# RWKV inverse in a hybrid retention and RWKV-7 block: both directions' units of a step inverted together, their matrix loaded by four transfers

## The chip, the cores and the metric

One core of one Trainium2 chip runs the kernel as one program. The core has a matrix engine (PE, with its weight loads PEld), a vector engine (DVE), an activation engine (ACT), a general engine (POOL) and a queue engine (SP) that here issues most DMAs; in the traces here each executes its own instructions in the order in which they stand in the built program. Time is device time in microseconds of the whole launch, the median of several runs; "the profiled execution" is a further run with the hardware profiler on, which has a time of its own.

## The reference: what is computed

A transformer block for 1024 latent tokens and 256 context tokens, width 1024: an FFN, a mixer of two parallel branches (retention with 4 heads of 128, and RWKV-7 with 8 heads of 64), a second FFN, a final norm. The branch that the change concerns is the RWKV scan. It runs in two directions (z = 0 and 1), over the context first and then over the latents with the state that the context left:

```python
def step(s, inp):
    rt, wt, kt, vt, at, bt = inp
    sa = jnp.einsum('zbhvk,zbhk->zbhv', s, at)
    s_new = s * wt[..., None, :] + sa[..., :, None] * bt[..., None, :] + vt[..., :, None] * kt[..., None, :]
    y = jnp.where(is_fwd, einsum(s_new, rt), einsum(s, rt))
    return s_new, y
```

The kernel computes it in chunks of 64 tokens. Within a chunk the recurrence through `sa` is a unit triangular system of 64 equations for each head, so every chunk needs the inverse of a 64 by 64 triangular matrix.

## The kernel before, in words

**Stages.** `tile_kernel` builds, in this order: the start and the first FFN; the RWKV projections (`rkv`); the RWKV scan (`recurrences`, L1073); the remaining projections of the mixer (`fill`, L1128, made of `qkvg`, L765, and `gates`, L796); the retentions (L1136); the output projections (`merge_rwkv`, `merge_ret`, `residual`, whose PSUM tiles are `rwps` and `ops`); the second FFN (PSUM tiles `p` and `psd`) and the final norm. The instructions are not run in that order: a scheduler places each engine's instructions when the program is built, by dependencies and by when it reckons buffers and engines free. An instruction of a later stage can thus stand among those of an earlier one, if its tiles have memory that is free.

**The scan.** There are 10 steps, each with two units (z = 0 and 1) of 128 tokens, so 20 units. A unit goes through three parts.
- `prep` (L868) loads r, k, v, kk and the decay of 128 tokens, forms two prefix products (`w`, `wi`, L893), the scaled operands `ar` and `bk`, and with 32 matmuls the Gram matrices `gps`; DVE masks them into `g` (L926, L930).
- `inverse` (L958) inverts the 32 diagonal blocks of 32 by 32 (8 heads, 2 chunks, 2 halves) by substitution. The blocks are copied from `g` to DRAM (`scr<-g`, L969, four transfers), and read back by one transfer of 512 KB (`invn<-scr`, L970), whose source has a first dimension of stride 0: the 32 blocks stand four times over the 128 partitions. Partition group j solves for the rows j, j+4, ... ACT copies those into `invx` (L972). Then 30 times two DVE operations, a product into `invt` (L976) and a sum into `invx` (L977). Four memsets write the diagonal (L980), and the result goes to DRAM (`scr<-invx`, L981) and back into `g` (`g<-scr`, L983).
- `join` (L985) makes the 64 by 64 inverse of two 32 by 32 ones: for each of two chunks e, 8 transposes (`tps`), an ACT copy, 8 products (`hps`), an ACT copy, 8 products (`xps`), and a DVE copy into `g` (L1002).
- `chain` (L1004) is the recurrence proper. For each chunk: `q` from the state S and from `wv` (L1018, L1020), an ACT copy, `u` with the inverse (L1025), an ACT copy, the state's update (L1030, POOL L1032, DVE L1034), and the output (L1037, L1039 or L1041). `readout` (L1044) normalises the outputs of a page that both directions have visited and stores them (L1071).

**Order and buffers of the scan.** `recurrences` prepares and inverts units 0, 1 and 2 ahead (`ready`), and behind step s the units 2s+3 and 2s+4. The tiles `ar`, `g`, `bt`, `wv` and `pc` have a ring of four buffers; the loads of `prep` have one buffer each; `invn`, `invx` and `invt` have two buffers each.

**The fill.** `qkvg` has 40 blocks of 24 matmuls (`fps`, L207 to L209): 16 with 512 tokens, 8 with 256, 16 with 512. `gates` has 32 blocks with 512 tokens. A block's weights come by two DMAs of 256 KB (`wraw`), which ACT and POOL split in two (L196, L197). Of a head's four blocks in `qkvg`, the first two (q and rk) are rotated with the tables `cos` and `sin` (L774, L789 to L793). The blocks' results go through a tile `gs` with two buffers.

**Memory.** The tiles of the scan are taken from the low end of the on-chip memory upwards, those of the fill from the high end downwards. In the built program the last tile of the scan (a small one of `readout`) ends at byte 163,040 of a partition, and the lowest tile of the fill (`cos`, 2 KB) begins at byte 165,376.

Of the kernel before, what the change touches and what calls it, by code (L numbers as in the profile page):

```python
# [11 lines left out]
F32 = mybir.dt.float32  # L12
F32R = mybir.dt.float32r
AF = mybir.ActivationFunctionType
ALU = mybir.AluOpType
PSUM = bass.MemoryType.PSUM

P = 128
# [823 lines left out]
def ab(c):  # L842

    return 0 if c % 2 else 64
# [6 lines left out]
class Rwkv(Mixer):  # L851
# [103 lines left out]
            nc.scalar.activation(wv[r, :, e], ps[r], AF.Copy)  # L955
        return {"p": p, "ar": ar, "g": g, "bt": bt, "wv": wv, "pc": pc}

    def inverse(self, g, eng, tmp):  # L958


        nc = self.nc
        d0, d1 = (self.scr.tile([2, 2, 8, 32, 32], F32, tag="scr%d" % i, name="scr%d" % i) for i in range(2))
        n = tmp.tile([P, 32, 32], F32, tag="invn", name="invn", bufs=2)
        x = tmp.tile([P, 8, 32], F32, tag="invx", name="invx", bufs=2)
        t = tmp.tile([P, 72], F32, tag="invt", name="invt", bufs=2)
        ef = [(e, f, slice(ab(e) + 32 * f, ab(e) + 32 * f + 32)) for e in range(2) for f in range(2)]
        blk = lambda e, r: g[r, e, :, :, r].rearrange("i a b t -> i (a b) t")
        for e, f, r in ef:
            nc.sync.dma_start(out=d0[f, e].rearrange("q i t -> i q t"), in_=blk(e, r))  # L969
        nc.sync.dma_start(out=n, in_=d0.rearrange("f e q i t -> (f e q) (i t)").unsqueeze(0).to_broadcast([4, 32, 1024]))  # L970
        for j in range(4):
            nc.scalar.activation(x[32 * j:32 * j + 32], n[32 * j:32 * j + 32, j::4], AF.Copy)  # L972
        for i in range(1, 31):
            w, m = 31 - i, (i + 3) // 4
            tv = t[:, :m * w].rearrange("q (r c) -> q r c", c=w)
            eng.tensor_tensor(out=tv, in0=x[:, :m, i:i + 1].to_broadcast([P, m, w]), in1=n[:, i:i + 1, i + 1:].to_broadcast([P, m, w]), op=ALU.mult)  # L976
            eng.tensor_tensor(out=x[:, :m, i + 1:], in0=x[:, :m, i + 1:], in1=tv, op=ALU.add)  # L977
        for j in range(4):
            r = slice(32 * j, 32 * j + 32)
            eng.memset(x[r].rearrange("q k t -> q (k t)")[:, j::36], 1.0)  # L980
            nc.sync.dma_start(out=d1[:, :, :, j::4].rearrange("f e q k t -> (f e q) k t"), in_=x[r])  # L981
        for e, f, r in ef:
            nc.sync.dma_start(out=blk(e, r), in_=d1[f, e].rearrange("q i t -> i q t"))  # L983

    def join(self, g, tmp, pq):  # L985

# [86 lines left out]
    def recurrences(self, ctx):  # L1073
        nc, tc = self.nc, self.tc
        pool = lambda nm, bufs, **k: ctx.enter_context(tc.tile_pool(name=nm, bufs=bufs, **k))
        tmp, ring, ct = pool("btmp", 1), pool("bring", 4), pool("bct", 2)
        self.scr = pool("bscr", 2, space=bass.MemoryType.DRAM)
        pp, pc = pool("bpp", 2, space=PSUM, side="right"), pool("bpc", 2, space=PSUM)
        items = [(s, z) for s in range(10) for z in range(2)]
        un, seen = {}, set()  # L1080

        def ready(i):
            s, z = items[i]
            un[i] = self.prep(s, z, ring, tmp, pp)
            self.inverse(un[i]["g"], nc.vector, tmp)

        for i in range(3):
            ready(i)
        late, joined = [], set()

        def join(i):
            if i in un and i not in joined:
                joined.add(i)
                self.join(un[i]["g"], tmp, pc)

        for s in range(10):
            old, ys, late, runs = late, [], [], []
            for z in range(2):
                u = un[2 * s + z]
                p, y = u["p"], None  # L1100
                if p < 8:
                    y = ct.tile([P, 512], F32, tag="y", name="y", bufs=2)
                    if p in seen:
                        nc.scalar.dma_start(out=y, in_=self.dram["y", p])
                    ys.append((p, y))
                runs.append(self.chain(u, z, y, p not in seen, s == 9, ct, pc))
                join(2 * s + z)
                next(runs[z])
            for p, y in old:
                self.readout(p, y, ct, pc)  # L1110
            for z, x in enumerate(runs):
                next(x)
                if z == 0:
                    join(2 * s + 2)
            for p, y in ys:
                if p in seen:
                    late.append((p, y))
                else:
                    nc.scalar.dma_start(out=self.dram["y", p], in_=y)
                    seen.add(p)  # L1120
            for i in (2 * s + 3, 2 * s + 4):
                if i < 20:
                    ready(i)
            join(2 * s + 3)
        for p, y in late:
            self.readout(p, y, ct, pc)
# [422 lines left out]
```

## Time and profile before

| | us |
|---|---|
| median of 3 runs (lowest, highest) | 3290.09 (3285.87, 3291.71) |
| profiled execution, its own time | 3270.48 |
| its span, first to last instruction | 3268.7 |
| first matmul of the scan's chain (L1018) | 1276.1 |
| first and last load of `invn` | 1302.6 and 2183.4 |
| last matmul of the fill (L209, `fps`) | 2249.2 |
| last matmul of the chain (L1037) | 2301.3 |
| first matmul of `rwps`, of `ops`, of the second FFN (`p`) | 2343.9, 2464.5, 2562.9 |

A row of a view names a line of the kernel, an engine, an operation and its tiles as "written<-read", with buffer numbers left out. "x600: 144/216/1962" is a count with the least, the median and the longest duration in ns. In a row of groups, "202.5, 340 |" is the busy time in us and the mean of one in ns. A row of a stretch of time gives its limits and length in us, then for each engine the busy time with the number of instructions, then the granted share of the matrix engine's clock, the share of the DMA engines' time and GB/s. A row of the chain of work (what ended last, followed back) gives start, length and what it was. Matmuls overlap in the records, so a busy matrix engine isn't one at its peak.

### The profile page before, as it was taken

To read this page: it belongs to the slowest core of one execution; us is meant where nothing else is said; L and a number is where in the kernel's file an instruction comes from. 1 tells how busy PE (TensorE), PEld (TensorE's weight loads), DVE (VectorE), ACT (ScalarE), POOL (GpSimd) and SP (SyncE) were. 2 spreads that over 40 slices of the span, in tenths; PEclk is the share of its full clock that TensorE was granted. 3 is DMA by queue.
4 is the path that set the end of the run, shared out by engine and by line. 5 is a ranking of instruction groups with operands and counts; after the bars stand their busy time and mean duration, and the time that the engine had idled before them with its cause. 6 is when DMAs were issued, how large, how long until landed. Compare 5 with 4: busy or idle time off the path is not lost.

```text
span 3268.7 us, 47408 instructions
## 1 busy us (share of the span) xinstructions
PE 3037.0 (93%) x17879; PEld 2525.8 (77%) x17879; DVE 2006.5 (61%) x3826; ACT 1050.2 (32%) x1790; POOL 950.0 (29%) x768
## 2 busy tenths in 40 slices
PE   8999999999999998788889888888899899999998
PEld 4888888888887786677667677777787688888877
DVE  4876666444448874788666766755766776675012
ACT  5211111111115474334333333333423533333221
POOL 2111111111113313333332322332223533333442
PEclk9999999999999998888888888798899899999999
DMA  5432222111116246556444444534545244448651
GB/s 207 135 94 91 90 91 81 40 39 39 33 39 233 92 174 202 131 154 173 120 121 110 120 131 110 166 92 124 160 152 163 84 140 146 132 136 288 229 174 61
DMA packets 504557, 416.57 MB, mean 127 GB/s; under 512 B 92264, under 2 KB 401448, under 8 KB 504328
## 3 DMA queue, kind: packets, MB, share of 16 engines
q1 hardware_dynamic: 487776, 401.65, 40.5%
q10 hardware_dynamic: 16552, 11.90, 1.2%
q8 instruction: 141, 2.31, 0.3%
q14 instruction: 88, 0.72, 0.1%
HBM read 309.89 MB, written 99.35 MB: 125 GB/s over the span
## 4 chain that ended last, share of the span: by engine, by line
PE 66%; DVE 15%; DMA 11%; issue 3%; ACT 2%; SPq 2%; POOL 1%; DVEq 0%; ACTq 0%; POOLq 0%
PE psd L207 5%; PE psd L208 5%; PE psd L209 5%; DMA invn<-scr 5%; PE p L208 4%; PE p L209 4%; PE p L207 4%; PE psg L209 3%; DVE invt L976 3%; PE psu L208 3%; PE psg L208 3%; PE psu L209 3%; PE psu L207 3%; PE psg L207 3%; DVE invx L977 2%
## 5 line engine op out<-in xcount | busy, mean ns | idle before, releaser
L197 POOL TENSOR_TENSOR wlo<-wraw,whi 128x512 fp32r<-128x512 f32 (+1 forms) x246 | 437.8, 1790 | 1333.0 <-ACT whi L196 1251.5
L389 DVE SCALAR_TENSOR_TENSOR h<-psd,g,h 128x512 f32<-128x512 f32 (+1 forms) x504 | 313.6, 657 | 273.0 <-PE psd L209 272.8
L196 ACT ACTIVATE whi<-wraw 128x512 fp32r<-128x512 f32 (+1 forms) x246 | 193.8, 804 | 369.3 <-DMA wraw<-in_w_in_dram 88.7
L207 PE MATMUL fps<-uh,whi 128*128 128x512 f32 (+1 forms) x576 | 247.3, 430 | 23.9 <-ACT whi L196 15.0
L207 PE MATMUL p<-v,fac 128*128 128x512 f32 x616 | 242.0, 393 | 11.2 <-ACT v L42 6.1
L209 PE MATMUL fps<-uh,wlo 128*128 128x512 f32 (+1 forms) x576 | 245.5, 427 | 3.3 <-POOL wlo L197 3.3
L208 PE MATMUL p<-v,fac 128*128 128x512 f32 x616 | 242.0, 393 | 4.6 <-DVE v L43 4.6
L208 PE MATMUL fps<-ul,whi 128*128 128x512 f32 (+1 forms) x576 | 243.5, 423 | 0.1
L976 DVE TENSOR_TENSOR invt<-invx,invn 128x60 f32<-128x60 f32 (+5 forms) x600 | 202.5, 340 | 66.1 <-issue 31.0
L209 PE MATMUL p<-v,fac 128*128 128x512 f32 x616 | 241.4, 392 | 0.0
L977 DVE TENSOR_TENSOR invx<-invx,invt 128x60 f32<-128x60 f32 (+5 forms) x600 | 193.6, 325 | 26.3 <-DMA rsw<-gs 6.0
L207 PE MATMUL psd<-hh,whi 128*128 128x512 f32 (+1 forms) x528 | 189.8, 360 | 7.0 <-DVE h L389 6.9
L207 PE MATMUL psg<-uh,whi 128*128 128x512 f32 (+1 forms) x528 | 188.8, 358 | 0.9 <-ACT whi L196 0.9
L208 PE MATMUL psg<-ul,whi 128*128 128x512 f32 (+1 forms) x528 | 189.1, 358 | 0.4 <-POOL ul L259 0.4
L209 PE MATMUL psg<-uh,wlo 128*128 128x512 f32 (+1 forms) x528 | 188.8, 358 | 0.0
L207 PE MATMUL psu<-uh,whi 128*128 128x512 f32 (+1 forms) x528 | 187.7, 356 | 0.2 <-ACT whi L196 0.2
L208 PE MATMUL psu<-ul,whi 128*128 128x512 f32 (+1 forms) x528 | 187.6, 355 | 0.0
L208 PE MATMUL psd<-hl,whi 128*128 128x512 f32 (+1 forms) x528 | 187.1, 354 | 0.0
L209 PE MATMUL psu<-uh,wlo 128*128 128x512 f32 (+1 forms) x528 | 187.1, 354 | 0.0
L209 PE MATMUL psd<-hh,wlo 128*128 128x512 f32 (+1 forms) x528 | 186.8, 354 | 0.0
L207 PEld LDWEIGHTS fps<-uh,whi 128*128 128x128 f32 x576 | 123.5, 214 | 53.0 <-ACT whi L196 17.4
L43 POOL TENSOR_TENSOR fac<-draw,fac 128x512 fp32r<-128x512 f32 x88 | 114.3, 1302 | 138.9 <-ACT fac L42 137.8
(365 smaller groups left out, 7059.6 us busy)
## 6 DMA issues: line engine op xcount, KB each, us to landing
wraw<-in_w_in_dram SPq DMA_DIRECT2D x144, 256.0 KB
modw<-in_w_mod_dram SPq DMA_DIRECT2D x112, 256.0 KB
fraw<-in_ffn_w_gate_dram SPq DMA_DIRECT2D x88, 256.0 KB
hd<-d_hid SPq DMA_DIRECT2D x44, 512.0 KB
draw<-in_ffn_w_down_dram SPq DMA_DIRECT2D x88, 256.0 KB
wraw<-in_ffn_w_gate_dram SPq DMA_DIRECT2D x22, 512.0 KB
wraw<-in_ffn_w_up_dram SPq DMA_DIRECT2D x22, 512.0 KB
wraw<-in_ffn_w_down_dram SPq DMA_DIRECT2D x22, 512.0 KB
```

The costliest lines, as they stand in the source:

```text
L43: eng.tensor_tensor(out=v[1], in0=x, in1=v[0].bitcast(F32), op=ALU.subtract)
L196: nc.scalar.activation(hi[:, s], raw, AF.Copy)
L197: nc.gpsimd.tensor_tensor(out=lo[:, s], in0=raw, in1=hi[:, s].bitcast(F32), op=ALU.subtract)
L207: mm(ps, w[0][:, ws], x[0][xs], start=start, stop=False)
L208: mm(ps, w[0][:, ws], x[1][xs], start=False, stop=False)
L209: mm(ps, w[1][:, ws], x[0][xs], start=False, stop=stop)
L389: nc.vector.scalar_tensor_tensor(out=hs, in0=ps, scalar=gates()[v][:, m:m + 1], in1=hs, op0=ALU.mult, op1=ALU.add)
L976: eng.tensor_tensor(out=tv, in0=x[:, :m, i:i + 1].to_broadcast([P, m, w]), in1=n[:, i:i + 1, i + 1:].to_broadcast([P, m, w]), op=ALU.mult)
L977: eng.tensor_tensor(out=x[:, :m, i + 1:], in0=x[:, :m, i + 1:], in1=tv, op=ALU.add)
```

## The change

`inverse` takes both units of a step. `invn`, `invx` and `invt` get one more dimension u of two, and each of the 60 substitution operations covers both units: 60 operations of double size for a step, where there were 120. `invn` keeps its size in all, with one buffer of 8 KB for two of 4 KB. `invx` and `invt` keep two buffers and double: 2 KB for 1 KB, and 576 bytes for 288, so the scan's tiles take 2 x (1024 + 288) = 2,624 bytes more of each partition. The load of `invn` becomes four transfers of 128 KB for each unit, one for each partition group, with 32 rows each. Copies, stores and memsets stay as they were for each unit, but the memsets are shared. `recurrences` prepares two whole steps ahead (units 0 to 3), and behind step s the step s+2 (units 2s+4 and 2s+5).

```diff
-    def inverse(self, g, eng, tmp):
+    def inverse(self, gs, eng, tmp):
...
-        n = tmp.tile([P, 32, 32], F32, tag="invn", name="invn", bufs=2)
-        x = tmp.tile([P, 8, 32], F32, tag="invx", name="invx", bufs=2)
-        t = tmp.tile([P, 72], F32, tag="invt", name="invt", bufs=2)
+        n = tmp.tile([P, 2, 32, 32], F32, tag="invn", name="invn")
+        x = tmp.tile([P, 2, 8, 32], F32, tag="invx", name="invx", bufs=2)
+        t = tmp.tile([P, 144], F32, tag="invt", name="invt", bufs=2)
...
-        nc.sync.dma_start(out=n, in_=d0.rearrange("f e q i t -> (f e q) (i t)").unsqueeze(0).to_broadcast([4, 32, 1024]))
-        for j in range(4):
-            nc.scalar.activation(x[32 * j:32 * j + 32], n[32 * j:32 * j + 32, j::4], AF.Copy)
+        for u, g in enumerate(gs):
...
+            for j in range(4):
+                nc.sync.dma_start(out=n[32 * j:32 * j + 32, u].rearrange("q i t -> q (i t)"), in_=d0.rearrange("f e q i t -> (f e q) (i t)"))
+            for j in range(4):
+                nc.scalar.activation(x[32 * j:32 * j + 32, u], n[32 * j:32 * j + 32, u, j::4], AF.Copy)
         for i in range(1, 31):
             w, m = 31 - i, (i + 3) // 4
...
-            eng.tensor_tensor(out=x[:, :m, i + 1:], in0=x[:, :m, i + 1:], in1=tv, op=ALU.add)
+            eng.tensor_tensor(out=x[:, :, :m, i + 1:], in0=x[:, :, :m, i + 1:], in1=tv, op=ALU.add)
...
-        def ready(i):
-            s, z = items[i]
-            un[i] = self.prep(s, z, ring, tmp, pp)
-            self.inverse(un[i]["g"], nc.vector, tmp)
-
-        for i in range(3):
-            ready(i)
+        def ready(s):
+
+            for z in range(2):
+                un[2 * s + z] = self.prep(s, z, ring, tmp, pp)
+            self.inverse([un[2 * s + z]["g"] for z in range(2)], nc.vector, tmp)
+
+        ready(0)
+        ready(1)
...
-            for i in (2 * s + 3, 2 * s + 4):
-                if i < 20:
-                    ready(i)
+            if s < 8:
+                ready(s + 2)
```

In the built program of the change the last tiles of the scan (small tiles of `readout`, and 32 bytes of the second buffer of its tile `ysq`) end at byte 165,664; `cos`, the lowest tile of the fill, still begins at 165,376. The two share 288 bytes. The order in which the scheduler then places the instructions differs from the order before at the places below.

On SP, where `cos` is loaded for the first time: before, among the last stores of the RWKV projections (`d_td`, `d_na`, `d_r`), ahead of the scan's first unit.

```order
L717 DMA d_r<-rs 128x1024
L680 DMA d_td_66<-l2o 128x2x256
L774 DMA cos<-in_cst_cos_dram 128x512
L774 DMA sin<-in_cst_sin_dram 128x512
L194 DMA wraw<-in_w_in_dram 128x4x128
```

On SP in the change, the same load (L989 is the last return of an inverse to `g`, L1296 reads what `readout` stored).

```order
L987 DMA scr_15358<-invx 256x1x32 x2
L989 DMA g<-scr_15358 32x8x32 x4
L1296 DMA t_20089<-d_rw_83 128x128
L1296 DMA t_20089<-d_rw_86 128x128
L1296 DMA t_20089<-d_rw_89 128x128
L194 DMA wraw<-in_w_rwkv_o_dram 128x4x256 x4
L194 DMA wraw<-in_w_ret_o_dram 128x4x256
L774 DMA cos<-in_cst_cos_dram 128x512
L774 DMA sin<-in_cst_sin_dram 128x512
L789 DMA rsw<-gs 32x512
```

The load of `cos`, and with it all that follows it in `qkvg`, has moved from ahead of the scan to behind its last inverse.

On PE, in the middle of the scan before: a chain's `q` (L1018, L1020), a join (L998, L1001, L995) and a `prep` (L923), with matmuls of the fill (`fps`) between them.

```order
L1018 MATMUL q<-S_10082,ar 128x128 x4
L1020 MATMUL q<-wv,g 64x64 x3
L998 MATMUL hps<-tt,g 32x32 x8
L1020 MATMUL q<-wv,g 64x64 x5
L923 MATMUL gps<-ar,bk 128x128 x8
L207 MATMUL fps<-uh,whi 128x512
L208 MATMUL fps<-ul,whi 128x512
L209 MATMUL fps<-uh,wlo 128x512
```

On PE in the change, the same kind of place (lines of `join` and `chain` are six higher: L1024 and L1026 are `q`, L1004, L1007 and L1001 the join).

```order
L1024 MATMUL q<-S_10082,ar 128x128 x4
L1026 MATMUL q<-wv,g 64x64 x5
L923 MATMUL gps<-ar,bk 128x128 x8
L1007 MATMUL xps<-g,tt 32x32 x8
L1001 MATMUL tps<-ident,g 32x32 x8
L1026 MATMUL q<-wv,g 64x64 x3
L1004 MATMUL hps<-tt,g 32x32 x8
L947 MATMUL btps<-ident,bk 128x128 x8
```

On PE in the change, the end of the scan (L1043 is the chain's output, L1069 the readout).

```order
L1031 MATMUL u<-qa,g 64x64 x16
L1043 MATMUL q<-wv,g 64x64 x16
L1069 MATMUL ytps<-ident,y 128x128 x8
L207 MATMUL fps<-uh,whi 128x512
L208 MATMUL fps<-ul,whi 128x512
L209 MATMUL fps<-uh,wlo 128x512
```

In the change no `fps` stands between the first `q` and the last readout: 48 of the fill's 1,728 (two blocks) stand ahead of the scan, and 1,680 behind it.

On SP in the change, between one pair's substitution and the next (L974 loads `invn`, L987 and L989 store and return the pair before, L972 copies `g` of the next pair's second unit).

```order
L974 DMA invn<-scr_12901 32x1024
L987 DMA scr_12308<-invx 256x1x32 x4
L987 DMA scr_12322<-invx 256x1x32 x2
L989 DMA g<-scr_12308 32x8x32 x4
L987 DMA scr_12322<-invx 256x1x32 x2
L974 DMA invn<-scr_12901 32x1024 x2
L989 DMA g<-scr_12322 32x8x32 x4
L974 DMA invn<-scr_12901 32x1024
L972 DMA scr_12915<-g 32x8x32 x4
L974 DMA invn<-scr_12915 32x1024 x4
```

The next pair's first load stands ahead of the stores of the pair before, and its second unit's copy and loads behind their return. On DVE the second unit's masks (L926) stand behind the first join's copies (L1008) of the pair before.

More of the change, by code (lines that the diff above doesn't have):

```diff
@@ L956, in prep @@
         return {"p": p, "ar": ar, "g": g, "bt": bt, "wv": wv, "pc": pc}
-    def inverse(self, g, eng, tmp):
+    def inverse(self, gs, eng, tmp):
         nc = self.nc
-        d0, d1 = (self.scr.tile([2, 2, 8, 32, 32], F32, tag="scr%d" % i, name="scr%d" % i) for i in range(2))
-        n = tmp.tile([P, 32, 32], F32, tag="invn", name="invn", bufs=2)
-        x = tmp.tile([P, 8, 32], F32, tag="invx", name="invx", bufs=2)
-        t = tmp.tile([P, 72], F32, tag="invt", name="invt", bufs=2)
+        n = tmp.tile([P, 2, 32, 32], F32, tag="invn", name="invn")
+        x = tmp.tile([P, 2, 8, 32], F32, tag="invx", name="invx", bufs=2)
+        t = tmp.tile([P, 144], F32, tag="invt", name="invt", bufs=2)
@@ L966, in inverse @@
         ef = [(e, f, slice(ab(e) + 32 * f, ab(e) + 32 * f + 32)) for e in range(2) for f in range(2)]
[L967 to L970, printed above, removed]
-        for j in range(4):
-            nc.scalar.activation(x[32 * j:32 * j + 32], n[32 * j:32 * j + 32, j::4], AF.Copy)
+        blk = lambda g, e, r: g[r, e, :, :, r].rearrange("i a b t -> i (a b) t")
@@ new lines, in inverse @@
+        d1s = []
+        for u, g in enumerate(gs):
+            d0, d1 = (self.scr.tile([2, 2, 8, 32, 32], F32, tag="scr%d%d" % (u, i), name="scr%d" % i) for i in range(2))
+            d1s.append(d1)
+            for e, f, r in ef:
+                nc.sync.dma_start(out=d0[f, e].rearrange("q i t -> i q t"), in_=blk(g, e, r))
+            for j in range(4):
+                nc.sync.dma_start(out=n[32 * j:32 * j + 32, u].rearrange("q i t -> q (i t)"), in_=d0.rearrange("f e q i t -> (f e q) (i t)"))
+            for j in range(4):
+                nc.scalar.activation(x[32 * j:32 * j + 32, u], n[32 * j:32 * j + 32, u, j::4], AF.Copy)
@@ L973, in inverse @@
         for i in range(1, 31):
             w, m = 31 - i, (i + 3) // 4
-            tv = t[:, :m * w].rearrange("q (r c) -> q r c", c=w)
-            eng.tensor_tensor(out=tv, in0=x[:, :m, i:i + 1].to_broadcast([P, m, w]), in1=n[:, i:i + 1, i + 1:].to_broadcast([P, m, w]), op=ALU.mult)
-            eng.tensor_tensor(out=x[:, :m, i + 1:], in0=x[:, :m, i + 1:], in1=tv, op=ALU.add)
+            tv = t[:, :2 * m * w].rearrange("q (u r c) -> q u r c", u=2, c=w)
+            eng.tensor_tensor(out=tv, in0=x[:, :, :m, i:i + 1].to_broadcast([P, 2, m, w]), in1=n[:, :, i:i + 1, i + 1:].to_broadcast([P, 2, m, w]), op=ALU.mult)
@@ L978, in inverse @@
+            eng.tensor_tensor(out=x[:, :, :m, i + 1:], in0=x[:, :, :m, i + 1:], in1=tv, op=ALU.add)
         for j in range(4):
             r = slice(32 * j, 32 * j + 32)
[L980 to L983, printed above, removed]
+            eng.memset(x[r].rearrange("q u k t -> q u (k t)")[:, :, j::36], 1.0)
@@ L985, in join @@
+        for u, g in enumerate(gs):
+            for j in range(4):
+                nc.sync.dma_start(out=d1s[u][:, :, :, j::4].rearrange("f e q k t -> (f e q) k t"), in_=x[32 * j:32 * j + 32, u])
+            for e, f, r in ef:
+                nc.sync.dma_start(out=blk(g, e, r), in_=d1s[u][f, e].rearrange("q i t -> i q t"))
     def join(self, g, tmp, pq):
@@ L1078, in recurrences @@
         pp, pc = pool("bpp", 2, space=PSUM, side="right"), pool("bpc", 2, space=PSUM)
-        items = [(s, z) for s in range(10) for z in range(2)]
         un, seen = {}, set()
-        def ready(i):
-            s, z = items[i]
-            un[i] = self.prep(s, z, ring, tmp, pp)
-            self.inverse(un[i]["g"], nc.vector, tmp)
-        for i in range(3):
-            ready(i)
+        def ready(s):
[4 more added lines that the diff above has]
+        ready(1)
         late, joined = [], set()
```

## The prediction

> **What bounds the kernel now.** I read the stretches of time first: they cut the span where the fill ends, where the first output projection starts and where the second FFN starts.
>
> ```profile
> 1276.00:2249.00 973.00, 836.88 (x6908) 693.97 (x6908) 678.39 (x1784) 345.73 (x669) 332.73 (x328) 0.85 0.48 129
> 2249.00:2344.00 95.00, 72.29 (x674) 65.66 (x672) 61.37 (x175) 41.31 (x79) 26.20 (x18) 0.82 0.52 161
> 2344.00:2563.00 219.00, 206.79 (x1003) 171.51 (x1003) 142.31 (x262) 74.88 (x113) 75.07 (x37) 0.98 0.49 153
> 2563.00:3269.00 706.00, 679.44 (x3000) 561.07 (x3000) 352.86 (x476) 240.66 (x396) 261.26 (x194) 0.97 0.48 156
> ```
>
> The scan and the fill share 973 us. The matrix engine looks 86% busy there, but its records overlap, so next comes the chain of work over 1276 to 2301 us, then the inverse's tiles and its transfers.
>
> ```profile
> by line: DMA invn<-scr 14.8%; DVE invt L976 9.0%; DVE invx L977 7.9%; issue 5.8%; PE fps L207 3.8%; PE fps L209 3.7%; PE fps L208 3.5%; PE gps L923 2.5%; PE u L1025 2.2%; PE q L1018 2.2%; PE q L1020 2.2%; ACT invx L972 1.8%; DMA scr<-g 1.6%
> L976 DVE TENSOR_TENSOR invt<-invx,invn x600: 144/216/1962, 1316.4 to 2222.0; 128x60 f32<-128x60 f32 x30, 128x48 f32<-128x48 f32 x19, 128x28 f32<-128x28 f32 x18, 128x52 f32<-128x52 f32 x10
> L970 SPq DMA_DIRECT2D invn<-scr x20: 562/576/632, 1302.6 to 2183.4; - x20
> 1302.60 12.03 DMA invn<-scr
> 1340.61 11.27 DMA invn<-scr
> ```
>
> The chain's largest item is the load of `invn`, 12.03 us from issue to landing; the substitution follows. The matrix multiplications of the fill have 3.5 to 3.8% a line: the stage is paced by the scan's latency, and the fill runs in its holes. 20 loads lie between 1302.6 and 2183.4 us, 46.4 us a unit, so a step takes 92.7 us before. That the fill costs nothing of its own is what the kernel before lives on.
>
> **The change part by part.** What decides is not in the substitution. The scan's tiles now reach 288 bytes into the place of `cos`, so `cos` is loaded when the last readout has done with that memory. The first head's q and rk blocks hold both `gs` buffers until they are rotated with `cos`; so after two blocks the fill stands, and the order of PE shows it: 48 of 1,728 matmuls ahead of the scan, none in it, 1,680 behind. The rest follows from three durations: the scan alone, the fill alone, and the tail.
>
> *The scan alone: a step.* Its DVE work comes first.
>
> ```profile
> L976 DVE TENSOR_TENSOR invt<-invx,invn 128x60 f32<-128x60 f32 (+5 forms) x600 | 202.5, 340 | 66.1 <-issue 31.0 <-ACT invx L972 16.2 <-DMA wraw<-in_w_in_dram 3.9
> L977 DVE TENSOR_TENSOR invx<-invx,invt 128x60 f32<-128x60 f32 (+5 forms) x600 | 193.6, 325 | 26.3 <-DMA rsw<-gs 6.0 <-issue 4.6
> L926 DVE TENSOR_TENSOR g<-gps,c_msk 128x512 f32<-128x512 f32 x64 | 43.0, 686 | 5.5 <-PE gps L923 4.6
> L1034 DVE TENSOR_TENSOR S<-S,u 64x256 f32<-64x256 f32 x70 | 29.1, 416 | 11.1 <-PE u L1030 9.8
> L793 DVE TENSOR_TENSOR gs<-gs,rsw 128x512 f32<-128x512 f32 x16 | 17.3, 1081 | 0.0
> L1002 DVE COPY g<-xps 32x256 f32<-32x256 f32 x38 | 15.8, 416 | 38.0 <-PE xps L1001 31.2 <-issue 6.2
> L792 DVE TENSOR_TENSOR gs<-gs,cos 128x512 f32<-128x512 f32 x16 | 15.2, 948 | 15.5 <-ACT invx L972 8.9 <-DMA rsw<-gs 4.0 <-DMA wraw<-in_w_in_dram 2.5
> ```
>
> An operation of the substitution has a median of 216 ns and a least of 144, which is nearly all fixed cost. Twice the elements add about the difference: 288 ns, between 216 and 432. A pair takes 60 x 0.288 = 17.3 us; before, 120 operations took 120 x 0.216 = 25.9 us, and by the means 39.6. So the edit itself saves 8.6 to 22 us of DVE a step. The rest of DVE is 678.4 - 202.5 - 193.6 - 17.3 - 15.2 (the fill's own) = 249.8 us, 25.0 a step. Of it two state updates (0.8), four masks (2.7) and four copies of the join (1.7) stand between two substitutions by the order of DVE. The stretch from the start to the end of a substitution is thus 17.3 + 25.0 - 5.2 = 37.1 us.
>
> Between two substitutions nothing overlaps, because `invn` has one buffer now, and because the second unit's masks stand behind the first join.
>
> ```profile
> L969 SPq DMA_DIRECT2D scr<-g x80: 318/443/2003, 1299.1 to 2180.2; - x80
> L981 SPq DMA_DIRECT2D scr<-invx x80: 549/588/2413, 1354.9 to 2224.7; - x80
> 1274.16 3.37 DMA rsw<-gs
> 1357.30 1.92 DMA scr<-invx
> 1359.69 2.23 DMA g<-scr
> 1614.67 3.47 DMA wraw<-in_w_in_dram
> 1621.00 1.97 DMA rsw<-gs
> 1651.42 1.64 DMA scr<-g
> 2251.68 0.69 PE L998 MATMUL hps<-tt,g 32*32 32x32 f32 x16
> 2259.70 1.05 PE L998 MATMUL hps<-tt,g 32*32 32x32 f32 x16 [3.84 <-ACT tt L996]
> 2259.28 0.36 ACT L996 ACTIVATE tt<-tps 32x256 f32<-32x256 f32 x1
> 2262.97 0.41 DVE L1002 COPY g<-xps 32x256 f32<-32x256 f32 x1
> ```
>
> One load's issue (0.58), four stores (4 x 0.588), their landing (1.92), and the return (2.23, and one issue more) make 7.5 us. The join of a chunk took 2263.38 - 2259.28 = 4.1 us from the first ACT copy on, where no fill stood between, and its transposes 0.7: two chunks 9.6. Then state and masks 3.5, the copies of `g` 4 x 0.443 + 1.64 = 3.4, four loads 4 x 0.576 + landing, ACT 0.4. The new load is not in the trace; it lies between a 64-KB transfer (1.97 to 3.37) and the 512-KB one (12.03). I take 3 us for the last 128 KB, near the 256-KB weights (3.47). Sum: 7.5 + 9.6 + 3.5 + 3.4 + 2.3 + 3 + 0.4 = 29.7 us.
>
> [...]
>
> A step takes 37.1 + 29.7 = 67 us, for 92.7 before. The bounds are DVE's bare work (42) and 92.7.
>
> *The scan's place.* Its first `q` is at 1276 as before. The first substitution needs two units: between 1302.6 and 1340.6 for the last load; I take 1322. It starts at 1325 and ends at 1362, the tenth nine steps later: 1362 + 9 x 67 = 1965.
>
> ```profile
> L1018 PE MATMUL q<-S,ar x320: 272/275/582, 1276.1 to 2291.9; 128*128 128x128 f32 x128, 128*64 128x128 f32 x32
> 2284.75 2.07 PE L1018 MATMUL q<-S,ar 128*128 128x128 f32 x8 [2.52 <-DVE y L1041]
> 2288.76 0.59 ACT L1022 ACTIVATE qa<-q 64x512 f32<-64x512 f32 x1 [2.17 <-PE q L1020]
> 2271.74 2.97 DMA y<-d_bv
> 2274.84 1.27 POOL ysq L1070
> ```
>
> From there to the fill's restart: the joins of both units (7.5 + 2 x 9.6 = 27); one and a half chunks of chain (three matmul groups of 1 to 2 us, two ACT copies of 0.6, the state's sum 0.8: 7 each) and the last readout's arithmetic, 21 in all as an estimate from such pieces; its two loads and POOL products (8.5) and its store (3); `cos` with the first rotation (11). That is 70 us, bounds 50 and 100. The fill restarts at 2035.
>
> The new wait sits in SP's queue: behind `cos` stand the rotation's transfers, the weights of `qkvg` and all stores of its blocks, and on PE everything from the third block on. Nobody in the scan waits for it. No cover is left for the fill: it must be paid after the scan.
>
> *The fill alone.* No stretch shows it; the nearest is `ops`, 16 blocks of the same 24 matmuls with streamed weights.
>
> ```profile
> L207 PE MATMUL ops<-uh,whi x128: 388/389/628, 2464.5 to 2557.0; 128*128 128x512 f32 x128
> L209 PE MATMUL fps<-uh,wlo x576: 274/389/796, 1261.9 to 2249.2; 128*128 128x512 f32 x171, 128*128 128x256 f32 x21
> L207 PE MATMUL p<-v,fac x616: 387/389/792, 2562.9 to 3000.1; 128*128 128x512 f32 x154
> 1529.69 4.24 DMA ul<-d_u
> ```
>
> (2557.0 - 2464.5) / 16 = 5.8 us a block. Two blocks ran ahead, two more fit in PSUM while `cos` is awaited: 60 wide blocks make 348 us, 8 of half width 35 (23 to 46), three changes of the token group, whose operands come in transfers of some 4 us, 8 each. Sum 407, bounds 375 and 450: to 2442.
>
> *The tail.* Before, 2249.2 to 2562.9 = 314 us lay between the last `fps` and the second FFN, of which the chain and its readouts held a part up to 2344; from there it was 219. Now these are over earlier, and the retentions, which need the fill, remain: 255. The second FFN starts at 2697 and takes its 706: the end is at 3403, 134 us behind 3268.7. Against the profiled execution's own 3270.5 that is 3405; the median of the runs shown is 19.6 above it, so 3290 + 134 = 3424.
>
> **The rivals.** *Cold matrix engine, slower still.* Alone, the scan leaves it long pauses: the same 16 matmuls took 0.69 us behind dense work and 1.05 after 3.84 us of idling, and the clock granted in the scan is 0.85 even with the fill. If chain and masks wait for it too, 10 to 15 us a step come on top: 9 x 12 = 108, 3532. [...]
>
> *Faster.* A substitution saves more than the fill then costs, if a step alone takes under 67 - 134 / 9 = 52 us: stores, joins and loads must hide beneath DVE's 42 us. At 47 the time is 3290 + 134 - 180 = 3244. For it: long waits of the step before are those for the fill's matmuls in front. Against: one `invn` buffer, and SP's and DVE's order above.
>
> *The fill is not displaced*, as the diff alone reads: then 25.7 us a step are saved, 9 x 25.7 = 231, 3059. The order of PE excludes it all but wholly.
>
> **How the numbers follow.** Forecast 0.77; cold 0.14; faster 0.06; not displaced 0.01; 0.02 for a step near 52 us, which ends within 0.2% (6.6 us, about what a measurement here can tell from no change). Steps of 60 and 73 us move the forecast by 60, the fill by 35, tail and start by 30 each: together some 90. The range goes 114 down to 3310 and 106 up, to the cold case at 3530. Faster 0.07, same 0.02, slower 0.91.
>
> **What would show it.** `fps` must be absent between the first `q` and the last readout, with the matrix engine under half busy there; the loads of `invn` must recur every 67 us and land within about 4; `cos` must be issued near 2020; `fps` then runs dense for 400 us. I am wrong if a step is under 52 us, or if `fps` ends before 2330.

## The result, and the profile after

The changed kernel takes 3513.1 us (median of four runs, 3508.1 to 3525.8), the kernel before 3288.0 on the same chip: 1.070 times as long, 95% interval 1.065 to 1.075. The forecast was 3424, in a range of 3310 to 3530: the time lies inside it, near its upper end, and the kernel is 225 us slower where 134 were forecast. The profiled execution has a span of 3508.9 us, for 3268.7 before.

The stretches of time of the changed kernel, cut at the end of the scan's matmuls, the return of the fill, its end, and the start of the second FFN (start:end, length, busy time of PE, PEld, DVE, ACT and POOL, granted TensorE clock, DMA share, GB/s):

```profile
1276.00:2071.00 795.00, 558.33 (x5607) 502.19 (x5604) 454.10 (x1135) 231.83 (x467) 145.22 (x183) 0.59 0.30 75
2071.00:2097.00 26.00, 2.21 (x9) 1.43 (x8) 14.34 (x31) 5.38 (x9) 11.90 (x7) 0.56 0.55 169
2097.00:2537.00 440.00, 402.23 (x1732) 324.96 (x1733) 41.24 (x52) 122.96 (x216) 204.21 (x153) 0.94 0.54 166
2537.00:2803.00 266.00, 239.58 (x1247) 203.52 (x1246) 166.48 (x362) 97.21 (x162) 79.98 (x40) 0.95 0.45 143
2803.00:3509.00 706.00, 679.28 (x3000) 560.95 (x3000) 351.69 (x476) 240.55 (x396) 260.90 (x194) 0.97 0.48 156
```

Before, scan and fill shared 973 us. Now the scan has 795 for itself, in which TensorE gets 0.59 of its clock, and behind it the fill takes 440 at 0.94. The last stretch is as long as before, to the microsecond.

The instructions of the inverse, of `cos` and of the fill in the changed kernel (count, least, median and greatest duration in ns, first and last start):

```profile
L974 SPq DMA_DIRECT2D invn<-scr x80: 312/420/1423, 1296.5 to 1973.0; - x80
L980 DVE TENSOR_TENSOR invt<-invx,invn x300: 179/264/1974, 1318.5 to 2005.1; 128x120 f32<-128x120 f32 x30, 128x56 f32<-128x56 f32 x20, 128x96 f32<-128x96 f32 x20, 128x60 f32<-128x60 f32 x10
L774 SPq DMA_DIRECT2D cos<-in_cst_cos_dram x2: 333/336/340, 2096.5 to 2187.6; - x2
L207 PE MATMUL fps<-uh,whi x576: 278/389/797, 1261.4 to 2536.8; 128*128 128x512 f32 x171, 128*128 128x256 f32 x21
```

`cos` is loaded at 2096.5, behind the scan, and the `fps` matmuls end at 2537 where they ended at 2249. An operation of the pair has a median of 264 ns for twice the elements (216 before). How little of it goes with the elements, single operations of the kernel before show: 0.17 us with 8 elements a partition (at 1642.59), 0.23 with 68 (at 1719.51). Two waits in the scan changed places (engine and line, what it waited for, total, times, longest). In the kernel before:

```profile
ACT invx L972 <- DMA invn<-scr: 155.2, 19, 15.2
DVE g L1002 <- PE xps L1001: 31.2, 12, 7.2
```

and in the changed kernel:

```profile
DVE g L1008 <- PE xps L1007: 101.7, 23, 10.2
ACT invx L976 <- DMA invn<-scr: 64.8, 42, 8.4
```

ACT's copies wait 64.8 us for the load of `invn`, where they waited 155.2. DVE's copies of the join wait 101.7 us for TensorE, where they waited 31.2.

### The profile page after: what moved, and what is told of

Same layout as the page of the kernel before. It is cut to its first block, busy times and chain, and to the rows that moved or that the text cites. A ratio compares the mean times of both kernels' runs of the same rounds, so it can differ in the third digit from the quotient of the medians.

```text
span 3508.9 us, 46957 instructions
## 1 busy us (share of the span) xinstructions
PE 3121.0 (89%) x17879; PEld 2625.1 (75%) x17879; DVE 1798.3 (51%) x3186; ACT 1045.0 (30%) x1783; POOL 956.9 (27%) x768
## 3 DMA queue, kind: packets, MB, share of 16 engines
q1 hardware_dynamic: 488976, 401.65, 37.1%
## 5 line engine op out<-in xcount | busy, mean ns | idle before, releaser
L207 PE MATMUL fps<-uh,whi 128*128 128x512 f32 (+1 forms) x576 | 228.0, 397 | 42.9 <-ACT whi L196 21.9
L209 PE MATMUL fps<-uh,wlo 128*128 128x512 f32 (+1 forms) x576 | 226.2, 393 | 8.2 <-POOL wlo L197 8.0
L208 PE MATMUL fps<-ul,whi 128*128 128x512 f32 (+1 forms) x576 | 226.1, 393 | 0.9 <-DMA ul<-d_u 0.7
L207 PEld LDWEIGHTS fps<-uh,whi 128*128 128x128 f32 x576 | 114.4, 199 | 72.4 <-ACT whi L196 28.8
L923 PE MATMUL gps<-ar,bk 64*128 64x128 f32 (+1 forms) x640 | 99.4, 400 | 66.5 <-POOL ar L905 26.6
L1038 POOL TENSOR_TENSOR S<-S,pc 64x256 f32<-64x256 f32 x76 | 56.5, 743 | 332.5 <-PE q L1024 303.2
```

Source lines behind the costliest of these rows:

```text
L207: mm(ps, w[0][:, ws], x[0][xs], start=start, stop=False)
L208: mm(ps, w[0][:, ws], x[1][xs], start=False, stop=False)
L209: mm(ps, w[1][:, ws], x[0][xs], start=False, stop=stop)
L923: nc.tensor.matmul(pss[h][:, j, e, xs], bk[r, h0 + j, e], ar[r, h0 + j, e, xs], start=True, stop=True)
L1038: nc.gpsimd.tensor_tensor(out=S[hc[h], :, hc[h]], in0=S[hc[h], :, hc[h]], in1=pc[hc[h], e::2].unsqueeze(2).to_broadcast([64, 4, 64]), op=A ...
```

## The experiments

Two theories stood against each other at first. *Displacement*: the time is lost because 288 bytes push the fill out of the scan. *The pair*: the paired inverse with its one `invn` buffer is slow of itself. "First to last substitution" is the time from the first start of an `invt` operation to the last, and holds nine steps and most of a tenth.

**1. The change, made to fit.** One buffer of `invt`, which should make nothing wait, since DVE alone writes and reads it, one operation behind the other:

```diff
-        t = tmp.tile([P, 144], F32, tag="invt", name="invt", bufs=2)
+        t = tmp.tile([P, 144], F32, tag="invt", name="invt")
```

> The changed kernel with one buffer of invt instead of two: 576 bytes less a partition, so that the scan's last tiles end at byte 165,088, below the start of cos (165,376); the order of PE has 1,668 fps matmuls inside the scan again. Displacement theory (what costs is that the fill is pushed behind the scan, by 288 bytes): the time falls below the kernel before. PE then sets the pace: about 400 us of fps and some 430 us of the scan's own matmuls at a full clock, 830 to 880 us between the first q and the last, where before has 973: 3290 - 100 = about 3190 us, between 3140 and 3240. Rival (the paired inverse with its one invn buffer is slow of itself): 3290 us or more, up to 3510.

3177.1 us, 0.9686 of the kernel before (0.9672 to 0.9700). Its `fps` and its substitutions:

```profile
L207 PE MATMUL fps<-uh,whi x576: 278/389/795, 1262.3 to 2092.6; 128*128 128x512 f32 x171, 128*128 128x256 f32 x21
L980 DVE TENSOR_TENSOR invt<-invx,invn x300: 171/274/1837, 1339.0 to 2171.8; 128x120 f32<-128x120 f32 x30, 128x56 f32<-128x56 f32 x20, 128x96 f32<-128x96 f32 x20, 128x60 f32<-128x60 f32 x10
```

The fill runs through the scan again and is done by 2093. The `invt` operations wait for ACT (10.8 us) and for two loads (6.1 us), and for no operation of DVE. The scan is longer than where it runs alone (832.8 us from first to last substitution, for 686.6), and still the kernel is some 335 us faster than the changed one. Displacement is what costs.

**2. The kernel before, made not to fit.** Padding alone, no instruction more:

```diff
-        t = tmp.tile([P, 72], F32, tag="invt", name="invt", bufs=2)
+        t = tmp.tile([P, 400], F32, tag="invt", name="invt", bufs=2)
```

> The kernel before with invt padded from 72 to 400 elements, so that its scan tiles end at byte 165,664 like those of the changed kernel; not one instruction is added. Displacement theory: fps leaves the scan, cos is issued behind the last readout, and the time is 150 to 300 us above the kernel before: 3440 to 3590 us (the scan alone 75 to 85 us a step, then 430 us of fps as in the changed kernel). Rival (the paired inverse is what costs): within 1% of the kernel before, 3260 to 3320 us.

3561.0 us, 1.0856 (1.0833 to 1.0879).

```profile
L774 SPq DMA_DIRECT2D cos<-in_cst_cos_dram x2: 333/336/340, 2140.7 to 2233.0; - x2
L207 PE MATMUL fps<-uh,whi x576: 277/389/796, 1262.9 to 2584.0; 128*128 128x512 f32 x171, 128*128 128x256 f32 x21
```

`cos` comes late and `fps` ends 335 us later than before. The same displacement, without any of the change, costs 283 us.

**3 and 4. Where the step is.** The same padding, with 364 and with 360 elements for 400: an overlap of 32 bytes, and a gap of 32.

> The kernel before with invt padded from 72 to 364 elements: the scan's last tile ends at byte 165,408, 32 bytes above the start of cos. Displacement as a step (any overlap displaces the whole fill): the same time as with 288 bytes of overlap, 3540 to 3580 us. Rival (the price grows with the bytes, or is one of the padding itself): between the kernel before and that, under 3450 us.

> The kernel before with invt padded from 72 to 360 elements: the scan's last tile ends at byte 165,344, 32 bytes below the start of cos, and TensorE's order is word for word that of the kernel before. Displacement as a step: 3265 to 3295 us, as the kernel before. Rival (the padding has a price of its own, from other addresses): over 3310 us.

364 elements: 3559.3 us, 1.0867 (1.0836 to 1.0898). 360 elements: 3280.1 us, 1.000 (0.9982 to 1.0018). The price is a step: 32 bytes cost what 288 cost, and the padding itself nothing.

**5. The load alone.** The kernel before, with only the load in four transfers:

```diff
-        nc.sync.dma_start(out=n, in_=d0.rearrange("f e q i t -> (f e q) (i t)").unsqueeze(0).to_broadcast([4, 32, 1024]))
+        for j in range(4):
+            nc.sync.dma_start(out=n[32 * j:32 * j + 32].rearrange("q i t -> q (i t)"), in_=d0.rearrange("f e q i t -> (f e q) (i t)"))
```

> The kernel before with only the load of invn in four transfers. If the broadcast's 10 to 12 us is on the path while the fill runs beside it, some 8 us a unit go, less what PE's queue takes back: 3200 to 3270 us. Rival (the load is hidden behind the other unit's substitution and the wait for PE): within 0.5% of the kernel before, 3275 to 3305 us.

3174.2 us, 0.9680 (0.9665 to 0.9695): better than either theory had it, and not to be told from the fitting change.

```profile
L977 DVE TENSOR_TENSOR invt<-invx,invn x600: 154/216/1964, 1301.9 to 2089.4; 128x60 f32<-128x60 f32 x29, 128x48 f32<-128x48 f32 x19, 128x28 f32<-128x28 f32 x13, 128x70 f32<-128x70 f32 x10
```

First to last substitution takes 787.5 us here and took 905.6 before: 118 us gone, of which the time shows 104. The load was on the path even with the fill beside it.

**6. The pair with the old load.** The fitting kernel of experiment 1, with one broadcast transfer for each unit:

```diff
-            for j in range(4):
-                nc.sync.dma_start(out=n[32 * j:32 * j + 32, u].rearrange("q i t -> q (i t)"), in_=d0.rearrange("f e q i t -> (f e q) (i t)"))
+            nc.sync.dma_start(out=n[:, u].rearrange("q i t -> q (i t)"), in_=d0.rearrange("f e q i t -> (f e q) (i t)").unsqueeze(0).to_broadcast([4, 32, 1024]))
```

> The fitting kernel (one buffer of invt) with the old broadcast load, one for each unit. If the load is on the path once the fill runs beside it: 5 to 8 us more a step than the fitting kernel, so 50 to 80 us above it. Rival (PE is full in the scan and hides the load): within 0.5% of the fitting kernel.

3322.1 us, 1.0127 (1.0111 to 1.0142): 145 us above experiment 1, about twice what was expected, and slower than the kernel before. ACT's wait for the load, here:

```profile
ACT invx L975 <- DMA invn<-scr: 185.5, 20, 13.6
```

and in experiment 1:

```profile
ACT invx L976 <- DMA invn<-scr: 47.9, 37, 6.9
```

138 us more of waiting stand beside 145 us more of time. That fits a load which, in a pair, nothing covers.

**7. The pair alone, where the scan runs alone.** The padding of experiment 2 and the load of experiment 5 together; against the changed kernel the pairing is undone, and with it the order in which units are prepared and the one buffer of `invn`.

> The kernel before with both the padded invt (400 elements, the scan's tiles end at byte 165,664 as in the changed kernel) and the load in four transfers: against the changed kernel only the pairing of the substitution is undone. If the pairing pays where the scan runs alone (it takes 8 to 22 us of DVE a step): 3540 to 3561 us, little below the padded kernel. Rival (in the scan alone the short load is worth as much as the pairing, since the load is on the path and a single unit starts earlier): 3470 to 3520 us, at or below the changed kernel's 3513.

3414.1 us, 1.0414 (1.0380 to 1.0448), below both ranges. The same stretch of time of this kernel:

```profile
1320.00:1920.00 600.00, 493.51 (x4983) 445.65 (x4983) 482.37 (x1653) 206.43 (x416) 118.34 (x155) 0.60 0.35 86
```

and of the changed kernel:

```profile
1320.00:1920.00 600.00, 418.50 (x4308) 375.44 (x4307) 350.62 (x888) 184.00 (x370) 102.11 (x136) 0.59 0.30 76
```

With single units DVE is busy 482 of 600 us, with pairs 351, at the same granted clock. The pair does its substitution in fewer operations and then lets DVE stand: in the scan alone it is 2.8% the worse (1.0703 / 1.0414), some 95 us. With the fill beside it (experiments 1 and 5), it gains nothing and loses nothing in the whole time.

The traces show where those 95 us lie. With single units, 15 of the 19 gaps between one substitution's last operation and the next one's first are under 1.5 us: while DVE solves one unit, the next is made ready. In the changed kernel the nine gaps are 35.9 us in the mean. Two units take 63.2 us with single units, and a pair takes 73.2.

**8 and 9. Is it the single buffer?** The prediction put the pair's gaps down to the one buffer of `invn`, and to the order of the second unit's masks. The changed kernel with two buffers (the fill is displaced anyway), and experiment 7 with one (padded to the same end):

```diff
-        n = tmp.tile([P, 2, 32, 32], F32, tag="invn", name="invn")
+        n = tmp.tile([P, 2, 32, 32], F32, tag="invn", name="invn", bufs=2)
```

> The changed kernel with two buffers of invn for one (8 KB more a partition; the fill is behind the scan anyway). The padded kernel before with the four-transfer load took 3414 us, so the pairing costs 99 us, 10 a step. If that is the single buffer of invn, as the prediction had it (the next pair can't be loaded before this substitution ends): 3410 to 3450 us. Rival (a pair can't begin before both its units are prepared, and no substitution runs beside the other unit's stores, return and join, whatever the buffers): 3490 to 3520 us.

> The padded kernel before with the load in four transfers (3414 us), and with one buffer of invn for two, the padding grown so that the scan's tiles end at the same byte. If the single buffer is what makes the pair slow: 3480 to 3520 us, as the changed kernel. Rival (the buffer matters little, a unit's load is only 3 to 5 us from issue to use): 3414 to 3450 us.

Two buffers for the pair: 3501.5 us, 1.0682 (1.0654 to 1.0710), an interval that overlaps that of the changed kernel. One buffer for the single units: 3560.1 us, 1.0853 (1.0833 to 1.0873), some 145 us more than experiment 7. In experiment 7 the next load goes out while a substitution runs (1596.3 to 1624.8); with one buffer it goes out when the substitution ends (1604.7). The load in experiment 7, then with one buffer:

```profile
1619.19 1.72 SPq L971 DMA_DIRECT2D invn<-scr  x4
```
```profile
1604.56 0.33 SPq L971 DMA_DIRECT2D invn<-scr  x1
```

With one buffer no gap between substitutions is under 6.8 us, and their mean is 10.1, for 3.2 with two. With pairs the second buffer buys hardly anything: the mean gap is 35.4 us with two and 35.9 with one. One step of the pair with two buffers, on SP and on DVE:

```profile
1606.43 0.83 SPq L974 DMA_DIRECT2D invn<-scr  x2
...
1644.55 1.78 SPq L972 DMA_DIRECT2D scr<-g  x4
1648.83 1.71 SPq L974 DMA_DIRECT2D invn<-scr  x4
```
```profile
1643.23 1.29 DVE L926 TENSOR_TENSOR g<-gps,c_msk 128x512 f32<-128x512 f32 x2 [2.54 <-PE gps L923]
1654.79 0.22 DVE L980 TENSOR_TENSOR invt<-invx,invn 128x60 f32<-128x60 f32 x1 [2.96 <-ACT invx L976]
```

The first unit is loaded at 1606, while the pair before is still being solved: that is what the buffer allows. The second unit's last mask is done at 1644.5, its blocks are copied and loaded behind that, and the pair starts at 1654.8. It starts when its second unit is there. So the theory of the buffer falls for the pair. What stands is the prediction's other reason, the place of the second unit's masks: with two buffers too they come behind the joins of the pair before. No experiment moves those masks alone.

**10 and 11. Is it the cold clock?** Matmuls that nobody reads were added to the changed kernel so that TensorE has work while it waits: 64 of 128 x 128 behind each load of `invn` and 24 behind each substitution; then 24 and 12.

```diff
+        def spin(src, k):
+            ps = pp.tile([P, 4, P], F32, tag="mm", name="spin")
+            for h in range(k):
+                nc.tensor.matmul(ps[:, h % 4], self.K.ident, src, start=True, stop=True)
+        for h in range(4):
+            spin(n[:, 1, 4 * h:4 * h + 4].rearrange("q i t -> q (i t)"), 16)
...
+        spin(x[:, 1, :4].rearrange("q k t -> q (k t)"), 24)
```

> The changed kernel with matrix multiplications added whose results nobody reads, 64 of 128 x 128 behind each load of invn and 24 behind each substitution, so that TensorE is busy where it waits. Theory (the step is 73 us and not 67 because TensorE runs at half its clock behind the pauses: 8 matmuls of 128 x 128 take 2.07 us there and 1.16 at the full clock): the granted clock rises well above 0.59 in the scan, the step falls by 4 to 10 us, the time to 3420 to 3480 us. Rival (the clock is no matter, the step waits for transfers and DVE): 3505 to 3560 us, the added matmuls only stand in the way.

> As the kernel with added matrix multiplications before (88 a step: granted clock 0.80 in the scan but 3551 us, with PE so full that they stood in the way), with 36 a step: 24 behind each load of invn, 12 behind each substitution, about the pause that the stores and the return leave. Theory (the cold clock costs some 6 us a step): 3440 to 3490 us if the clock rises to 0.70 or more. Rival (the clock doesn't matter, or can't be had without delaying the rest): 3500 to 3550 us.

88 a step: 3550.9 us, 1.0823 (1.0775 to 1.0870). 36 a step: 3542.8 us, 1.0795 (1.0773 to 1.0818). The first of the two, in the stretch of experiment 7:

```profile
1320.00:1920.00 600.00, 539.53 (x5704) 500.43 (x5703) 336.01 (x859) 179.92 (x363) 97.40 (x129) 0.80 0.29 72
```

The clock rose from 0.59 to 0.80, and the scan became no shorter: first to last substitution takes 706.3 us for 686.6. The stretch of a substitution fell from 36.4 to 27.6 us in the mean, and the gap before the next grew from 35.9 to 48.0. The added matmuls stand in TensorE's order in front of the chain's, which would explain the gap. In the second the clock rose to 0.64 only (from 1320 to 1990 us, where the first has 0.80 too), less than the 0.70 that its expectation asked for. These runs don't settle what the cold clock costs; they show only that it can't be bought off in this way.

**Together.** The four corners with the fill in the scan, and three of those with the fill behind it:

| inverse, load | fill in the scan | fill behind it |
|---|---|---|
| single units, broadcast | 1 (the kernel before) | 1.0856 |
| single units, four transfers | **0.9680** | 1.0414 |
| pairs, broadcast | 1.0127 | not run |
| pairs, four transfers | 0.9686 | 1.0703 (the change) |

Two kernels beat both the kernel before and the change: the kernel before with the short load, and the change with one buffer of `invt`. The first is the simpler.

## Why the prediction was right, and where it was not

**The cause: right, and shown.** Experiments 1 to 4 show it from both sides. `fps` is absent from the scan, and `cos` waits for the last readout. The end of that readout in the changed kernel, on POOL, on SP, on ACT and on TensorE:

```profile
2091.07 2.48 POOL L1076 TENSOR_TENSOR ysq<-ysq,y 128x512 f32<-128x512 f32 x2
```
```profile
2096.47 0.34 SPq L774 DMA_DIRECT2D cos<-in_cst_cos_dram  x1
```
```profile
2092.36 1.58 ACTq L1077 DMA_DIRECT2D d_rw<-ysq  x2
2096.36 1.09 ACT L785 ACTIVATE gs<-fps 128x512 f32<-128x512 f32 x2 [10.38 <-DMA d_rw<-ysq]
```
```profile
2097.01 0.79 PE L207 MATMUL fps<-uh,whi 128*128 128x512 f32 x1 [12.53 <-ACT gs L785]
```

The last store of `ysq` is issued by 2093.9 and has landed by 2096.4. Within a microsecond `cos` is issued and the fill's third block starts.

One detail of the mechanism was otherwise. The prediction had the first two blocks in the `gs` buffers, held there until they are rotated with `cos`. By the rows above, ACT copies these blocks out of PSUM into `gs` only at 2096.36, behind the landing of that same store, and TensorE's third block waits for that copy and not for the rotation. So no block more ran ahead while the fill stood.

**The sum: too small in four terms of six.** The end was forecast at 3403 and came at 3509.

| term | forecast | measured | difference |
|---|---|---|---|
| first substitution ends | 1362 | 1350.6 | -11 |
| nine steps | 603 | 655 | +52 |
| from there to the fill's return | 70 | 91.5 | +22 |
| the fill alone | 407 | 440.3 | +33 |
| tail | 255 | 265.5 | +10 |
| second FFN and end | 706 | 706 | 0 |

"Measured" goes from the last operation of one stage to that of the next. The tenth substitution ends at 2005.5, `fps` returns at 2097.0 and ends at 2537.3, the second FFN starts at 2802.8.

The errors are nearly all of one sign, so hardly anything cancelled: the way and the mechanism were right, and the size was 106 us short.

*The step* is the largest miss: 73.2 us by the starts of the first and the tenth substitution (1318.5 and 1977.3), for 67. The substitution itself was nearly right (18 to 21 us of busy time for 17.3, stretches of 36.4 for 37.1 in the mean), the load too. In the first pair, four transfers are issued from 1296.49 on, and ACT's last copy of them starts at 1302.06:

```profile
1296.49 1.70 SPq L974 DMA_DIRECT2D invn<-scr  x4
```
```profile
1302.06 0.41 ACT L976 ACTIVATE invx<-invn 32x256 f32<-32x256 f32 x1 [0.98 <-DMA invn<-scr]
```

That is 5.6 us, for a forecast of 2.3 + 3; the broadcast took 12.03 from its issue to its landing. That the new load would be short was the author's estimate, and the rows bear it out; why four transfers of 128 KB are in sooner than one of 512 KB, no run here shows.

The term that was too small is the gap: 29.7 forecast, 35.9 measured (from a substitution's last operation to the next one's first, in the mean of nine). One gap, of 38 us, on TensorE and on DVE:

```profile
1632.20 1.06 PE L1001 MATMUL tps<-ident,g 32*32 32x32 f32 x16 [9.83 <-DMA g<-scr]
1640.36 1.97 PE L1031 MATMUL u<-qa,g 64*64 64x64 f32 x16
1646.98 2.08 PE L1024 MATMUL q<-S,ar 128*128 128x128 f32 x8
1650.24 2.08 PE L923 MATMUL gps<-ar,bk 64*128 64x128 f32 x16
```
```profile
1626.14 0.21 DVE L984 MEMSET invx<- 32x16 f32 x2
1640.46 0.41 DVE L1008 COPY g<-xps 32x256 f32<-32x256 f32 x1 [3.70 <-PE xps L1007]
1652.35 1.29 DVE L926 TENSOR_TENSOR g<-gps,c_msk 128x512 f32<-128x512 f32 x2 [4.96 <-PE gps L923]
1664.15 0.22 DVE L980 TENSOR_TENSOR invt<-invx,invn 128x60 f32<-128x60 f32 x1 [2.91 <-DMA in_v<-d_v]
```

Stores and return take 6.1 us (1626.1 to 1632.2; forecast 7.5). Then the forecast had joins, state and masks for 13.1 us; here the last mask is done at 1653.6, 21.4 us later. In that time TensorE does the chain's `u`, `q` and `gps`, one group behind another, and the masks wait for them. The forecast priced the joins as if TensorE had nothing else to do there. The granted clock is 0.50 in this gap (below). If the work from 1640.4 to 1653.6 shrank as eight 128 x 128 matmuls do at the full clock (1.16 us for 2.08), it would be 5.8 us shorter: an estimate, and near the whole miss. How much of the miss is TensorE's order and how much its clock stays open.

*To the fill's return.* The last step's `y` is asked for on ACT's queue behind the loads of the readouts before it. DVE waits for it, and TensorE for DVE (ACT's queue, DVE, TensorE):

```profile
2049.49 1.58 ACTq L1075 DMA_DIRECT2D y<-d_g  x2
2053.84 0.34 ACTq L1110 DMA_DIRECT2D y<-d_y  x1
```
```profile
2056.72 0.68 DVE L1047 TENSOR_TENSOR y<-y,q 64x512 f32<-64x512 f32 x1 [8.94 <-DMA y<-d_y]
```
```profile
2057.46 2.08 PE L1024 MATMUL q<-S,ar 128*128 128x128 f32 x8 [11.92 <-DVE y L1047]
```

These 12 us weren't in the 70; the other 10 are not broken down here, nor is the tail's miss.

*The fill alone* was forecast from blocks that never wait, and with 60 wide blocks left. It had 62, since none ran ahead into PSUM: by the forecast's 5.8 us a block, 12 us more. In the changed kernel, from 2097 to 2538 (busy, mean ns, idle before with its causes):

```profile
L207 PE MATMUL fps<-uh,whi 128*128 128x512 f32 (+1 forms) x560 | 220.9, 396 | 41.2 <-ACT whi L196 21.9 <-ACT gs L785 12.5 <-DMA uh<-d_u 6.6
L209 PE MATMUL fps<-uh,wlo 128*128 128x512 f32 (+1 forms) x560 | 219.3, 393 | 8.2 <-POOL wlo L197 8.0
L207 PE MATMUL rwps<-rw,whi 128*128 128x512 f32 x19 | 7.4, 392 | 0.0
```

Without the 12.5 us ahead of the stretch, some 37 us are waits for weights and operands, and 57 matmuls of the output projection are done in between. Most of the waits (21.9 and 8.0 us) are for the weights' preparation on ACT and POOL.

**The rivals.** *Cold matrix engine* (3532) named the nearer time, by a price that the runs don't confirm: the clock was cold as it said (0.59 in the scan), but experiments 10 and 11 don't isolate its cost, and experiment 7 is 2.8% faster at the same clock (0.60). *Faster* needed a step under 52 us; a step took 73.2, and in the pair nothing hid the stores and joins. *Not displaced* was priced at 3059 by taking the scan alone with a free fill. Experiment 1 is that case: 3177, since with the fill beside it the scan takes 832.8 us from first to last substitution and not 686.6.

**The signs.** `fps` was absent from the scan, as the prediction asked, and then ran for 440 us, where it asked for some 400. `cos` came at 2096 and not near 2020. One sign failed: the matrix engine was to be under half busy in the scan, and it was busy for 558 of 795 us, at 0.59 of its clock.

**What the prediction did not see.** It credited the pairing with 8.6 to 22 us of DVE a step. DVE's busy time does fall. The engines of experiment 5 over the whole span:

```profile
PE 3002.7 (95%) x17879; PEld 2500.4 (79%) x17879; DVE 1985.6 (63%) x3826; ACT 1055.7 (33%) x1792; POOL 952.6 (30%) x768
```

and of experiment 1:

```profile
PE 3001.5 (95%) x17879; PEld 2499.3 (79%) x17879; DVE 1866.1 (59%) x3186; ACT 1047.9 (33%) x1786; POOL 954.1 (30%) x768
```

120 us less of DVE, and the same time. TensorE is busy for 95% of the span in both. From first to last substitution the pair takes 832.8 us for 787.5, while the fill ends at 2092.6 for 2181.2 (experiments 1 and 5): a longer scan and an earlier fill, with the same end. The gain of the change is in its load, which the prediction had only as a term of the gap.

## What to carry to other kernels

When a change enlarges a tile, compare where its neighbours in memory end with where the next stage's first tile begins: here 32 bytes of overlap move 1,680 matmuls and cost 8.7%. Before two units are made one operation, ask what the second unit's work was covering; saved busy time on an engine can be worth nothing: here 120 us less of DVE, with the fill in place, left the time as it was. Time each part of a change by itself: the four transfers alone are worth 3.2%; beside them the pairing is worth nothing with the fill in place and minus 2.8% without it.

## What was not expected of the hardware

The granted TensorE clock stayed at half through 22.7 us of unbroken work. The changed kernel in pieces of 4 us (start:end, length, busy PE, PEld, DVE, ACT, POOL, clock, DMA share, GB/s):

```profile
1640.00:1644.00 4.00, 4.00 (x54) 3.75 (x54) 0.41 (x1) 1.38 (x3) 0.00 (x0) 0.50 0.00 0
...
1660.00:1664.00 4.00, 3.14 (x30) 2.69 (x28) 0.07 (x1) 2.72 (x6) 0.00 (x0) 0.50 0.84 212
...
1668.00:1672.00 4.00, 4.00 (x55) 3.74 (x51) 3.77 (x11) 1.42 (x3) 1.65 (x2) 1.00 0.01 4
1676.00:1680.00 4.00, 0.81 (x14) 0.67 (x12) 3.84 (x12) 0.23 (x1) 0.00 (x0) 1.00 0.37 103
...
1684.00:1688.00 4.00, 4.00 (x25) 3.54 (x24) 3.82 (x9) 0.01 (x1) 2.02 (x3) 0.50 0.22 66
```

TensorE is busy without a break from 1640.4 to 1663.1, and its clock stays at 0.50. It is at 1.00 from 1668 to 1680, and at 0.50 again from 1684 to 1688, behind a pause of 3.8 us. Eight 128 x 128 matmuls took 2.08 us at 1646.98 and take 1.16 at the full clock:

```profile
1669.03 1.16 PE L1024 MATMUL q<-S,ar 128*128 128x128 f32 x8
```

What the release of the clock depends on, no run here shows.
